# The way out of an expert block issued two blocks later, the ranking behind the first gather, and gated values in two small buffers

## The chip, the core and the metric

The kernel runs on one core of one Trainium2 chip. Its engines run side by side, each with its own queue in program order: TensorE (PE) multiplies, VectorE (DVE) and ScalarE (ACT) work element by element, GpSimd (POOL) does little here, SyncE (SP) issues the transfers. The metric is the device time of one execution in microseconds. Before the change it is 1520.44 us, the median of three runs (1520.12 to 1522.35).

## The reference

A two-layer encoder trunk on 256 tokens of width 1024, in float32. Each layer adds to the residual stream `h` a token mixer, a cross attention over 256 memory tokens, and a feed-forward part; layer 0 has a dense one of width 2816, layer 1 a mixture of eight experts of width 3584, of which each token takes two:

```python
logits = (xt @ w_router).astype(jnp.float32)
top_vals, top_idx = lax.top_k(logits, TOP_K)
top_w = jax.nn.softmax(top_vals, axis=-1)
combine = jnp.sum(jax.nn.one_hot(top_idx, N_EXPERTS, dtype=jnp.float32) * top_w[..., None], axis=1)
y = jnp.zeros_like(xt)
for e in range(N_EXPERTS):
    y = y + combine[:, e:e + 1] * swiglu(xt, w_gate[e], w_up[e], w_down[e])
```

with `swiglu(x) = (silu(x @ w_gate) * (x @ w_up)) @ w_down`. The expert weights are 352 MB, and every one of them is read once; that part takes more than half of the time.

## The kernel before, in words

**Weights.** They arrive in chunks of 1 MB (128 x 2048 float32), a chunk per DMA, into a buffer of the pool R (22 buffers of that size). Each chunk is split in two: ACT rounds it to `hi` (L196), DVE subtracts for `lo` (L197), both in R. Activations are split in the same way. A product is then three matmuls, hi·hi, hi·lo and lo·hi (in a small expert block two, since there the two halves of the activations stand side by side in one operand). The splits run up to four chunks ahead of PE, in five pairs of buffers; transfers are issued up to seven chunks ahead of the splits (`do_split`, `get`, `dma`, L160 to L209), but each must wait until its buffer is free.

**Expert blocks.** The tokens of an expert are gathered by a matmul with a one-hot matrix (`gather`: `pg` on DVE at L1132, the matmuls at L1147, ACT and DVE move the result to `xg` at L276 and L278). Eight experts stand in eight places, each cut into 7 blocks of 512 columns. Four places (0, 5, 6, 7) are large, with 128 slots for tokens; four are small, with 64; which expert stands where is decided on the chip by `sort`. A block has four steps: the gate product (two chunks), the value product (two chunks), the gated values, and the way out, `down` (two chunks, added to two PSUM banks `acc`). All these products are recorded at L1202. Large and small blocks alternate (`merged`), after three large ones and up to three small ones at the end: 28 pairs, a cycle of which spans seven.

**From value product to way out.** In a large block ACT applies SiLU to the gate product, DVE multiplies in the value product (`a`, L1246), PE turns the result by four transposes (L1228, `hidden`). In a small block ACT copies both products out, PE turns each (L1226), DVE multiplies (L1256). Then `parts` makes the two halves `hl` of the gated values: ACT the rounded one, DVE the rest (L1266). `down` reads them as the standing operand.

**Order.** There is no scheduler: the instructions stand in each engine's queue as the code issues them. `Run.blocks` issues for block i: its gate product, `hidden` of block i−1, its value product with `parts` of block i−1 in its middle, `gated`, and then the way out of block i−1. `chunks` lists the weight chunks in the order in which these steps take them. `later` holds small pieces (gather matmuls, adding a finished place to `h`) that are issued between the steps.

**The start of the experts.** `moe` gathers place 0 (`first`); after its first piece two splits, `weights` (the softmax of two) and `sort` (some twenty small DVE operations, L1027 to L1057) are issued, then the gather's other pieces. `sort` gives the numbers of the experts that stand in places 1 to 7, and their slots.

**Kept chunks.** The K product of layer 1's attention takes its weights partly from chunks that were loaded and split during layer 0's feed-forward part (`KEPT`, L423 to L434); a chunk holds two K blocks. The others come with the stream, split or not as the string `FULL` says; unsplit ones are multiplied at L461, one matmul of two passes, which the trace records as two.

Of the kernel before, what the change touches and what calls it, by code (L numbers as in the profile page):

```python
# [21 lines left out]
F32R = mybir.dt.float32r  # L22
# [7 lines left out]
P = 128  # L30
# [32 lines left out]
SPL = [(j * 512, min(512, FF - j * 512)) for j in range((FF + 511) // 512)]  # L63


KEPT = 3

R_BUFS = 22
M_BUFS = 8

SPLIT_BUFS, SPLIT_AHEAD = 3, 3
WIDE_BUFS, WIDE_AHEAD = 5, 8

WIDE_LOAD = 7

HALF = 64
SMALL = 4
LEAD = 3
# [4 lines left out]
def trunk(tc, x, xt_in, mem, mt_in, wa, wb, wc, wl0, wk1, wl1, wff, wmoe, cc, tk, moec, ident_d, gfin, out):  # L83
    nc = tc.nc
    PE, ACT, DVE, POOL = nc.tensor, nc.scalar, nc.vector, nc.gpsimd
    with contextlib.ExitStack() as c:
# [745 lines left out]
        def pe_later(n=1):  # L832
            for _ in range(n):
                if later:
                    later.pop(0)()
# [4 lines left out]
        def up(st, s, accs, mid=None):  # L840


            np_ = s.w // 128
            per = 1024 // s.w

            def part(i, wh, wl, t):
                for j in range(per):
                    k = i * per + j
                    w = slice(j * s.w, (j + 1) * s.w)
                    a, b = s.x(k, t)  # L850
                    mm3(accs[t][:, 0:s.w], a, b, wh[:, w], wl[:, w], k == 0, k == KC - 1)

            if mid:
                parts = st.many(np_)
                for t in range(NT):
                    for i in range(np_):
                        part(i, *parts[i], t)
                        if t == 0 and i == np_ // 2 - 1:
                            mid()
            else:  # L860
                for i in range(np_):
                    w = st.get()
                    for t in range(NT):
                        part(i, *w, t)
# [322 lines left out]
        class Block:  # L1187
# [7 lines left out]
            def product(self, x, out, items, first, last):  # L1195

                if self.small:
                    ops = [(x[:, f].rearrange("p i s -> p (i s)"), it[i]) for i in range(2) for f, *it in items]
                else:
                    ops = [(x[:, f, i], w) for f, wh, wl in items for i, w in ((0, wh), (0, wl), (1, wh))]  # L1200
                for i, (a, w) in enumerate(ops):
                    PE.matmul(out, a, w, start=first and i == 0, stop=last and i == len(ops) - 1)  # L1202

            def up(self, out, mid=None):
                for c in range(2):
                    if c and mid:
                        mid()
                    items = []
                    for i, (wh, wl) in enumerate(self.st.many(2)):
                        items += [(4 * c + 2 * i + q, wh[:, q * 512:(q + 1) * 512], wl[:, q * 512:(q + 1) * 512])  # L1210
                                  for q in range(2)]
                    self.product(self.place.xg, out, items, c == 0, c == 1)

            def copy(self, ps):
                m = M([P, 512], s="gu")
# [21 lines left out]
                    self.a = M([P, 512], s="a")  # L1237
                    ACT.activation(self.a, g, AF.Silu)  # L1238

            def value(self, mid=None):  # L1240
                u = mm()
                self.up(u, mid)
                if self.small:
                    self.u = self.copy(u)
                else:
                    DVE.tensor_tensor(self.a, u, self.a, op=OP.mult)  # L1246
# [12 lines left out]

            def parts(self):  # L1260
                n = self.place.n
                self.hl = (M if self.small else R)([P, 4, 2, n], F32R, s="hl")
                v = self.a.rearrange("p (f s) -> p f s", f=4)
                hi, lo = self.hl[:, :, 0], self.hl[:, :, 1]
                ACT.activation(hi, v, AF.Copy)
                DVE.tensor_tensor(lo, v, hi.bitcast(F32), op=OP.subtract)  # L1266

# [17 lines left out]
        class Run:  # L1285
# [14 lines left out]
            def blocks(self, st, steps, before):  # L1300

                fin = Final()
                prev = None
                todo = [Block(st, p, j) for p, j in steps]
                for i, b in enumerate(todo):
                    last = i == len(todo) - 1
                    if i in before:
                        before[i]()
                    if last:
                        fin.load()  # L1310
                    b.gate()
                    pe_later()
                    if prev:
                        prev.hidden()
                    pe_later()
                    b.value(prev and prev.parts)
                    pe_later()
                    b.gated()

                    def hidden():  # L1320
                        b.hidden()
                        b.parts()
                    if prev:
                        prev.down(hidden if last else None)
                    pe_later()
                    prev = b
                while later:
                    pe_later()
                table(AF.Sqrt)
                prev.down(end=lambda: fin.all(prev.place.part))  # L1330

        def merged():

# [7 lines left out]
        def chunks(order, at):  # L1341

            src = []
            for i, (p, j) in enumerate(order):
                src += [at(p, 6 * j + c) for c in range(4)]
                if i:
                    q, k = order[i - 1]
                    src += [at(q, 6 * k + c) for c in (4, 5)]
            q, k = order[-1]
            src += [at(q, 6 * k + c) for c in (4, 5)]  # L1350
            return [(a, 1024, (False, False)) for a in src]

        where = {}
# [12 lines left out]
        def moe(st, routed, weights, sort, combine):  # L1366
            slot, comb, slotp, combp, which, bases, nmax, r, saved = routed
            where["tile"] = which
            order = merged()
            run = Run(slotp, combp, r, saved)  # L1370
            places = [Place(run, p, 1 <= p <= SMALL) for p in range(NE)]

            places[0].run = Run(slot, comb, r, saved)
            st.wide = True
            first = places[0].gather()
            later.append(first.pop())
            later.append(combine)
            for i, f in enumerate(first):
                f()
                if i == 0:  # L1380
                    for _ in range(2):
                        st.do_split()
                    weights()
                    sort()
            st.ahead = WIDE_LOAD
            before = {}
            at = {x: i for i, x in enumerate(order)}

            def add(i, f):
                before.setdefault(i, []).append(f)  # L1390
            add(LEAD, run.save)
            for p in range(1, NE):
                add(max(1, at[p, 0] - 3), places[p].prepare)
            run.blocks(st, [(places[p], j) for p, j in order],
                       {i: lambda fs=fs: [f() for f in fs] for i, fs in before.items()})
# [70 lines left out]
        norm = mixer(1, st, kv1, norm, start1)  # L1466
        nxt = Norm(1, C_FFN, split=False)
        attention(1, st, kv1, norm, nxt)
        st.ahead = 6 * LEAD - 4
        routed, *pieces = route(nxt)  # L1470
        moe(st, routed, *pieces)

# [147 lines left out]
```

## Time and profile before

| what | value |
|---|---|
| median of three runs | 1520.44 us |
| profiled execution: time, span | 1520.13 us, 1518.4 us |
| PE busy | 1468.9 us, 97% |
| DVE busy, ACT busy | 1295.8 us, 85%; 1046.9 us, 69% |
| bytes moved, mean rate | 459 MB, 302 GB/s |
| expert chunks | 336 of 1 MB |

The experts begin at about 590 us and end with the span, and in this part the transfers run at 360 to 420 GB/s, so averages over the span say little about it. Stretches of it are read by themselves: "pair" is one large and one small block, about 30 us when nothing else is issued in it. The records of matmuls overlap: the start of one to the start of the next is what it costs PE, not its length. "Idle before" is what an engine waited just ahead of an instruction, with the instruction that released it.

### The profile page before, as it was taken

The page shows a single profiled execution, that of the slowest core. Times are in us where ns is not written, and L with a number is a line of the kernel's source. Part 1 is how long each engine was busy: PE and PEld are TensorE (multiplying, and loading weights), DVE is VectorE, ACT ScalarE, POOL GpSimd, SP SyncE. Part 2 cuts the span into 40 slices and gives each one's busy share as a digit, 9 for nine tenths or more (in the row PEclk, how much of TensorE's full clock was granted, in tenths as well). Part 3 has the DMA queues.
Part 4 walks back from the last instruction along what each step waited for, and adds up shares of the span by engine and source line. Part 5 has one row for each costly group of instructions (what it writes and reads, how often), then busy time and mean ns, then how long its engine had stood idle before and what let it go on. Part 6 is the DMA issues. An engine that isn't in the chain of part 4 may idle for free.

```text
span 1518.4 us, 20836 instructions
## 1 busy us (share of the span) xinstructions
PE 1468.9 (97%) x7773; PEld 1263.6 (83%) x7773; DVE 1295.8 (85%) x1498; ACT 1046.9 (69%) x1226; POOL 8.0 (1%) x23
## 2 busy tenths in 40 slices
PE   7999999999999998999999999999999999999996
PEld 7998988888999897888888778888777888777884
DVE  7988767555798867999998999998999998999996
ACT  7547574444653655788787878787878787878884
POOL 0000000000000001000000000000000000000000
PEclk9999999999999998999999999999999999999998
DMA  9625465544452547599999999999999999999991
GB/s 371 245 90 215 164 231 186 203 167 180 153 210 81 208 162 324 196 383 418 388 403 399 359 373 423 378 406 388 373 374 420 376 410 372 380 366 422 416 418 65
DMA packets 65327, 459.04 MB, mean 302 GB/s; under 512 B 7233, under 2 KB 7745, under 8 KB 11841
## 3 DMA queue, kind: packets, MB, share of 16 engines
q1 hardware_dynamic: 65216, 457.62, 75.9%
q8 instruction: 63, 1.03, 0.3%
q14 instruction: 48, 0.39, 0.1%
HBM read 456.55 MB, written 1.05 MB: 301 GB/s over the span
## 4 chain that ended last, share of the span: by engine, by line
PE 83%; DVE 8%; ACT 4%; issue 3%; DMA 0%; SPq 0%; DVEq 0%; ACTq 0%
PE mm L1202 26%; PE acc L1202 16%; PE mm L220 5%; PE mm L218 5%; PE mm L219 5%; DVE lo L197 5%; PE acc L219 3%; PE acc L220 3%; PE acc L218 3%; ACT hi L196 3%; PE z L219 2%; PE z L220 2%; PE z L218 2%; PE mm L461 2%; PE mm L490 2%
## 5 line engine op out<-in xcount | busy, mean ns | idle before, releaser
L197 DVE TENSOR_TENSOR lo<-w,hi 128x2048 fp32r<-128x2048 f32 (+3 forms) x504 | 943.6, 1913 | 57.5 <-ACT hi L196 50.6
L196 ACT ACTIVATE hi<-w 128x2048 fp32r<-128x2048 f32 (+3 forms) x504 | 795.0, 1616 | 108.8 <-DVE lo L197 36.5
L1202 PE MATMUL mm<-hi,xg 128*128 128x512 f32 x1344 | 409.9, 393 | 2.2 <-DVE xg L278 1.1
L1202 PEld LDWEIGHTS mm<-hi,xg 128*128 128x128 f32 x1344 | 250.6, 188 | 53.2 <-DVE xg L278 1.6
L1202 PE MATMUL mm<-lo,xg 128*128 128x512 f32 x896 | 294.5, 390 | 0.0
L1202 PE MATMUL acc<-hi,hl 128*128 128x512 f32 x672 | 219.1, 401 | 23.5 <-DVE hl L1266 23.5
L1202 PEld LDWEIGHTS mm<-lo,xg 128*128 128x128 f32 x896 | 168.3, 188 | 34.6
L1202 PEld LDWEIGHTS acc<-hi,hl 128*128 128x128 f32 x672 | 124.4, 189 | 60.5 <-DVE hl L1266 36.6
L1202 PE MATMUL acc<-lo,hl 128*128 128x512 f32 x448 | 157.4, 392 | 0.0
L1202 PEld LDWEIGHTS acc<-lo,hl 128*128 128x128 f32 x448 | 84.6, 189 | 17.0
L218 PE MATMUL z<-hi,xt 128*128 128x320 f32 (+1 forms) x256 | 78.4, 306 | 7.9 <-ACT xt L336 7.9
L219 PE MATMUL z<-lo,xt 128*128 128x320 f32 (+1 forms) x256 | 77.5, 303 | 0.1
L220 PE MATMUL z<-hi,xt 128*128 128x320 f32 (+1 forms) x256 | 77.5, 303 | 0.0
L546 DVE SCALAR_TENSOR_TENSOR ca<-ca,cct 128x256 f32<-128x256 f32 x180 | 77.1, 480 | 0.2
L218 PE MATMUL mm<-hi,xt 128*128 128x512 f32 (+1 forms) x192 | 71.8, 374 | 0.0
L220 PE MATMUL mm<-hi,xt 128*128 128x512 f32 (+1 forms) x192 | 71.4, 372 | 0.0
L219 PE MATMUL mm<-lo,xt 128*128 128x512 f32 (+1 forms) x192 | 71.3, 371 | 0.0
L1226 PEld LDWEIGHTS mm<-twice,gu 128*128 128x128 f32 x448 | 58.1, 191 | 3.9
L1238 ACT ACTIVATE a<-mm 128x512 f32<-128x512 f32 x28 | 16.7, 596 | 61.3 <-PE mm L1202 61.3
L1226 PE MATMUL mm<-twice,gu 128*128 128x64 f32 x448 | 56.1, 268 | 0.0
L218 PEld LDWEIGHTS z<-hi,xt 128*128 128x128 f32 x256 | 49.4, 193 | 8.0 <-ACT xt L336 7.9
L219 PEld LDWEIGHTS z<-lo,xt 128*128 128x128 f32 x256 | 49.4, 193 | 0.3 <-DVE lo L197 0.3
(284 smaller groups left out, 1929.7 us busy)
## 6 DMA issues: line engine op xcount, KB each, us to landing
w<-in_wmoe_dram SPq DMA_DIRECT2D x336, 1024.0 KB, 7.9
w<-in_wl_dram SPq DMA_DIRECT2D x39, 1024.0 KB, 4.9
w<-in_wff_dram SPq DMA_DIRECT2D x33, 1024.0 KB, 4.8
w<-in_wb_dram SPq DMA_DIRECT2D x8, 960.0 KB, 8.7
w<-in_wa_dram SPq DMA_DIRECT2D x5, 1024.0 KB, 6.0
w<-in_wc_dram SPq DMA_DIRECT2D x8, 640.0 KB, 5.1
tk<-in_tk_dram SPq DMA_DIRECT2D x2, 1024.0 KB, 10.9
mt<-in_mem_t_dram SPq DMA_DIRECT2D x2, 1024.0 KB, 11.8
```

The costliest lines, as they stand in the source:

```text
L196: ACT.activation(hi[:, ws], r, AF.Copy)
L197: DVE.tensor_tensor(lo[:, ws], r, hi[:, ws].bitcast(F32), op=OP.subtract)
L218: PE.matmul(ps, ah, bh, start=start, stop=False)
L219: PE.matmul(ps, ah, bl, start=False, stop=False)
L220: PE.matmul(ps, al, bh, start=False, stop=stop)
L461: PE.matmul(self.kps[:, d, :], w[:, ks], self.mt[:, k, :], start=k == 0, stop=k == KC - 1)
L490: PE.matmul(ps[:, t, :], self.mt[:, k, tok(t)], p_[:, w], start=k == 0, stop=k == KC - 1)
L546: return lambda: DVE.scalar_tensor_tensor(dst, src[:, k:k + S], w, dst, op0=OP.mult, op1=OP.add)
L1202: PE.matmul(out, a, w, start=first and i == 0, stop=last and i == len(ops) - 1)
L1226: PE.matmul(ps[:, f * n:(f + 1) * n], w, twice, start=True, stop=True)
L1238: ACT.activation(self.a, g, AF.Silu)
```

## The change

1. The order in `Run.blocks` and of the chunks in `chunks`: block i's gate product, `hidden` of block i−1, the way out of block i−2 with `parts` of block i−1 in its middle, block i's value product, `gated`. Two ways out are left at the end.
2. `sort` is issued behind all pieces of the first gather instead of behind the first one.
3. The halves of a large block's gated values stand in two buffers of the pool M instead of one of R. R has 21 buffers instead of 22, M (a quarter of the size) 12 instead of 8. Small blocks keep one M buffer.
4. Two K chunks are kept instead of three. By `FULL`, the two K blocks of the third, which now comes with the stream, are not split.
5. 14 instead of 16 chunks may be issued before the ranking (`6 * LEAD - 6`); they are those of place 0, which need no ranking. `PRESPLIT` names a number that stays 2.

Lines of the changed kernel are two higher (L1202 becomes L1204) and one higher from L1226 to L1246.

```diff
-KEPT = 3
-R_BUFS = 22
-M_BUFS = 8
+KEPT = 2
+R_BUFS = 21
+M_BUFS = 12
...
+PRESPLIT = 2
...
                 if self.small:
-                    ops = [(x[:, f].rearrange("p i s -> p (i s)"), it[i]) for i in range(2) for f, *it in items]
+                    ops = [(x[0][:, f].rearrange("p i s -> p (i s)"), it[i]) for i in range(2) for f, *it in items]
                 else:
-                    ops = [(x[:, f, i], w) for f, wh, wl in items for i, w in ((0, wh), (0, wl), (1, wh))]
+                    ops = [(x[i][:, f], w) for f, wh, wl in items for i, w in ((0, wh), (0, wl), (1, wh))]
...
             def parts(self):
                 n = self.place.n
-                self.hl = (M if self.small else R)([P, 4, 2, n], F32R, s="hl")
+                if self.small:
+                    t = M([P, 4, 2, n], F32R, s="hl")
+                    self.hl = t, None
+                    hi, lo = t[:, :, 0], t[:, :, 1]
+                else:
+                    hi, lo = self.hl = [M([P, 4, n], F32R, s="hl") for _ in range(2)]
                 v = self.a.rearrange("p (f s) -> p f s", f=4)
-                hi, lo = self.hl[:, :, 0], self.hl[:, :, 1]
...
                     b.gate()
                     pe_later()
-                    if prev:
-                        prev.hidden()
+                    if i:
+                        todo[i - 1].hidden()
+                    if i > 1:
+                        pe_later()
+                        todo[i - 2].down(todo[i - 1].parts)
+                    elif i:
+                        todo[i - 1].parts()
                     pe_later()
-                    b.value(prev and prev.parts)
+                    b.value()
                     pe_later()
                     b.gated()
-
-                    def hidden():
-                        b.hidden()
-                        b.parts()
-                    if prev:
-                        prev.down(hidden if last else None)
-                    pe_later()
-                    prev = b
+                b.hidden()
+                todo[-2].down(b.parts)
                 while later:
                     pe_later()
                 table(AF.Sqrt)
-                prev.down(end=lambda: fin.all(prev.place.part))
+                b.down(end=lambda: fin.all(b.place.part))
...
             for i, (p, j) in enumerate(order):
-                src += [at(p, 6 * j + c) for c in range(4)]
-                if i:
-                    q, k = order[i - 1]
+                src += [at(p, 6 * j + c) for c in (0, 1)]
+                if i > 1:
+                    q, k = order[i - 2]
                     src += [at(q, 6 * k + c) for c in (4, 5)]
-            q, k = order[-1]
-            src += [at(q, 6 * k + c) for c in (4, 5)]
+                src += [at(p, 6 * j + c) for c in (2, 3)]
+            for q, k in order[-2:]:
+                src += [at(q, 6 * k + c) for c in (4, 5)]
...
                 if i == 0:
-                    for _ in range(2):
+                    for _ in range(PRESPLIT):
                         st.do_split()
                     weights()
-                    sort()
+            sort()
...
-        st.ahead = 6 * LEAD - 4
+        st.ahead = 6 * LEAD - 6
```

On PE, around a small block in the middle of the experts (`xg_7552` before, `xg_7484` after are its tokens). Before: its gate product, the turn of the large block ahead of it (`a_7865`), its value product, the turn of its own gate (`gu_7976`), and the way out of the large block just turned (`hl_8006`):

```order
L1202 MATMUL mm_7947<-hi_7874,xg_7552 128x512 x4
...
L1202 MATMUL mm_7947<-lo_7896,xg_7552 128x512 x4
...
L1228 MATMUL mm_7982<-ident,a_7865 128x128 x4
...
L1202 MATMUL mm_7991<-hi_7914,xg_7552 128x512 x4
...
L1202 MATMUL mm_7991<-lo_7929,xg_7552 128x512 x4
...
L1226 MATMUL mm_8029<-twice,gu_7976 128x64 x4
L1202 MATMUL acc_7508<-hi_7948,hl_8006 128x512
L1202 MATMUL acc_7508<-lo_7949,hl_8006 128x512
```

After: the same steps, with the way out of the block before the turned one (`hl_7826`) between the turn and the value product:

```order
L1204 MATMUL mm_7885<-hi_7808,xg_7484 128x512 x4
...
L1204 MATMUL mm_7885<-lo_7830,xg_7484 128x512 x4
L1229 MATMUL mm_7916<-ident,a_7800 128x128 x4
L1204 MATMUL acc_6417<-hi_7848,hl_7826 128x512 x2
...
L1204 MATMUL acc_6418<-lo_7867,hl_7826 128x512 x2
L1204 MATMUL mm_7958<-hi_7886,xg_7484 128x512 x4
...
L1204 MATMUL mm_7958<-lo_7901,xg_7484 128x512 x4
...
L1227 MATMUL mm_7993<-twice,gu_7914 128x64 x4
L1204 MATMUL mm_8000<-hi_7921,xg_6845 128x512
```

The way out that follows the value product is gone from there; the next block's gate product (`mm_8000`) follows at once, and the turned block's own way out comes a block later.

On DVE, at the start of the experts. Before: two splits, the ranking (its first and last operation), the moves of place 0's tokens, three splits:

```order
L197 TENSOR_TENSOR lo_5751<-w_5557,hi_5750 128x2048
L1027 COPY t_5766<-mm_5695 128x8
...
L1057 CAST nmax<-t_5790 128x1
L278 SCALAR_TENSOR_TENSOR xg_5721<-mm_5796,cct,xg_5721 128x128 x4
L278 SCALAR_TENSOR_TENSOR xg_5721<-mm_5813,cct,xg_5721 128x128 x4
L197 TENSOR_TENSOR lo_5832<-w_5726,hi_5831 128x2048
```

After:

```order
L199 TENSOR_TENSOR lo_5709<-w_5519,hi_5708 128x2048
L280 SCALAR_TENSOR_TENSOR xg_5683<-mm_5724,cct,xg_5683 128x128 x4
L280 SCALAR_TENSOR_TENSOR xg_5683<-mm_5741,cct,xg_5683 128x128 x4
L1029 COPY t_5758<-mm_5657 128x8
...
L1059 CAST nmax<-t_5782 128x1
L199 TENSOR_TENSOR lo_5790<-w_5688,hi_5789 128x2048
```

The ranking has moved behind the eight moves and stands ahead of the third split.

## Rows read from the trace of the kernel before

**Rows 1.** Page, part 1: busy us, share of the span, instructions.

```profile
PE 1468.9 (97%) x7773; PEld 1263.6 (83%) x7773; DVE 1295.8 (85%) x1498; ACT 1046.9 (69%) x1226; POOL 8.0 (1%) x23
```

**Rows 2.** Page, part 5: busy us, mean ns, idle time before and its releaser.

```profile
L197 DVE TENSOR_TENSOR lo<-w,hi 128x2048 fp32r<-128x2048 f32 (+3 forms) x504 | 943.6, 1913 | 57.5 <-ACT hi L196 50.6
...
L1202 PE MATMUL acc<-hi,hl 128*128 128x512 f32 x672 | 219.1, 401 | 23.5 <-DVE hl L1266 23.5
```

**Rows 3.** Waits of PE, 620 to 1462 us: total us, times, longest.

```profile
PE acc L1202 <- DVE hl L1266: 20.3, 25, 1.6
```

**Rows 4.** Timeline of PE, 1453 to 1463.6 us: start, length, tile, count, idle before.

```profile
1453.25 1.07 PE L1202 MATMUL mm<-hi,xg 128*128 128x512 f32 x4
...
1456.88 0.60 PE L1228 MATMUL mm<-ident,a 128*128 128x128 f32 x4
...
1462.12 0.40 PE L1202 MATMUL acc<-lo,hl 128*128 128x512 f32 x1
1463.01 0.73 PE L1202 MATMUL acc<-hi,hl 128*128 128x512 f32 x2 [0.49 <-DVE hl L1266]
```

**Rows 5.** Timeline of DVE, 1450 to 1463 us.

```profile
1450.66 0.69 DVE L1246 TENSOR_TENSOR a<-mm,a 128x512 f32<-128x512 f32 x1
1451.26 11.09 DVE L197 TENSOR_TENSOR lo<-w,hi 128x2048 fp32r<-128x2048 f32 x5
1462.27 0.68 DVE L1266 TENSOR_TENSOR hl<-mm,hl 128x512 fp32r<-128x512 f32 x1
```

**Rows 6.** Timeline of PE after its wait at 1339.75 us.

```profile
1339.75 1.04 PE L1202 MATMUL acc<-hi,hl 128*128 128x512 f32 x2 [1.64 <-DVE hl L1266]
...
1343.50 0.63 PE L1202 MATMUL acc<-hi,hl 128*128 128x512 f32 x2
```

**Rows 7.** Windows: length, busy PE, PEld, DVE, ACT, POOL, PEclk, DMA share, GB/s.

```profile
629.50:660.90 31.40, 31.16 (x145) 25.63 (x144) 29.18 (x17) 26.18 (x19) 0.00 (x0) 1.00 0.96 366
755.20:981.50 226.30, 220.11 (x1066) 182.84 (x1064) 212.62 (x149) 180.94 (x149) 0.00 (x0) 1.00 0.97 390
1340.00:1344.00 4.00, 4.00 (x12) 3.10 (x12) 4.00 (x3) 0.06 (x1) 0.00 (x0) 0.57 0.40 170
1371.20:1401.50 30.30, 29.79 (x141) 24.62 (x140) 28.47 (x17) 24.74 (x19) 0.00 (x0) 1.00 1.01 421
1462.10:1478.50 16.40, 15.91 (x78) 13.11 (x76) 16.38 (x13) 13.33 (x13) 0.00 (x0) 1.00 1.01 422
```

**Rows 8.** Page, part 6: expert chunks, KB each, median us to landing.

```profile
w<-in_wmoe_dram SPq DMA_DIRECT2D x336, 1024.0 KB, 7.9
```

**Rows 9.** Waits of the DMA queue of SyncE, 620 to 1462 us.

```profile
SPq L170 <- PE mm L1202: 374.2, 134, 8.0
```

**Rows 10.** Timeline of DVE and ACT around the ranking and the first gather.

```profile
599.01 0.15 DVE L1027 COPY t<-mm 128x8 f32<-128x8 f32 x1
...
601.07 2.15 ACT L276 ACTIVATE xg<-mm,cct 128x128 fp32r<-128x128 f32 x8
...
602.95 2.15 DVE L278 SCALAR_TENSOR_TENSOR xg<-mm,cct,xg 128x128 fp32r<-128x128 f32 x8
...
618.95 0.53 DVE L1132 TENSOR_SCALAR pg<-mct,slotp,t 128x64 f32<-128x64 f32 x2
```

**Rows 11.** Timeline of PE there.

```profile
603.35 0.73 PE L1202 MATMUL mm<-hi,xg 128*128 128x512 f32 x2 [1.15 <-DVE xg L278]
...
619.60 3.68 PE L1147 MATMUL mm<-pg,h 128*128 128x64 f32 x32
```

**Rows 12.** Timeline of PE in layer 1's K product.

```profile
451.69 3.72 PE L461 MATMUL mm<-mt,w 128*128 128x256 f32 x16
455.06 0.47 PE L218 MATMUL mm<-ms,khi 128*128 128x256 f32 x1
...
456.20 0.28 PE L220 MATMUL mm<-ms,klo 128*128 128x256 f32 x1
456.32 0.28 PE L218 MATMUL mm<-ms,khi 128*128 128x256 f32 x1
```

More of the change, by code (lines that the diff above doesn't have):

```diff
@@ L1197, in product, with up @@
                 if self.small:
-                    ops = [(x[:, f].rearrange("p i s -> p (i s)"), it[i]) for i in range(2) for f, *it in items]
+                    ops = [(x[0][:, f].rearrange("p i s -> p (i s)"), it[i]) for i in range(2) for f, *it in items]
                 else:
-                    ops = [(x[:, f, i], w) for f, wh, wl in items for i, w in ((0, wh), (0, wl), (1, wh))]
+                    ops = [(x[i][:, f], w) for f, wh, wl in items for i, w in ((0, wh), (0, wl), (1, wh))]
                 for i, (a, w) in enumerate(ops):
                     PE.matmul(out, a, w, start=first and i == 0, stop=last and i == len(ops) - 1)
-            def up(self, out, mid=None):
+            def up(self, out):
                 for c in range(2):
-                    if c and mid:
-                        mid()
                     items = []
@@ L1211, in up @@
                                   for q in range(2)]
-                    self.product(self.place.xg, out, items, c == 0, c == 1)
+                    xg = self.place.xg
+                    self.product((xg, None) if self.small else (xg[:, :, 0], xg[:, :, 1]), out, items, c == 0, c == 1)
             def copy(self, ps):
@@ L1238, in gate, with value @@
                     ACT.activation(self.a, g, AF.Silu)
-            def value(self, mid=None):
+            def value(self):
                 u = mm()
-                self.up(u, mid)
+                self.up(u)
                 if self.small:
@@ L1302, in blocks @@
                 fin = Final()
-                prev = None
                 todo = [Block(st, p, j) for p, j in steps]
                 for i, b in enumerate(todo):
-                    last = i == len(todo) - 1
                     if i in before:
                         before[i]()
-                    if last:
+                    if i == len(todo) - 1:
                         fin.load()
```

## The prediction

> **What bounds the kernel now.** The page comes first: TensorE (PE) is busy for 97% of the span [rows 1], so time can only come from its gaps or from its matmuls' number and pace. Of the costly groups, only the matmuls of the way out, `acc<-hi,hl`, have much idle time ahead of them: 23.5 us, all put down to the subtraction `hl` of VectorE (DVE) at L1266 [rows 2]. The waits of PE, cut to the expert blocks between 620 and 1462 us, name nothing else: 25 waits, 20.3 us [rows 3]. So three questions remain: what one such wait costs, what would be late next, and what the other edits cost.
>
> The timeline of one pair of blocks answers the first. Four queued 128x512 matmuls take 1.07 us and a single one shows 0.39 (0.40 here), so they follow one another every (1.07 − 0.39)/3 = 0.227 us, and 0.165 of a record is the pipeline's tail [rows 4]. Around a wait the starts at 1462.12 and 1463.01 stand 0.89 us apart: lost are 0.89 − 0.23 = 0.66, where the bracket says 0.49. A wait of the list therefore costs its idle time and about 0.165 more. Its cause stands in the order: the gated values of the block before are turned only after the next block's gate product, ScalarE (ACT) and DVE make their two parts in the middle of its value product, DVE ends `hl` at 1462.95 [rows 5], and the first matmul that reads it is due at 1462.35.
>
> What would be late next: in a cycle of seven pairs of blocks (755.20 to 981.50) the span is 226.3 us. DVE is busy for 212.6 and the transfers run at 390 GB/s. The bare pair at 1371.20 runs at 421 GB/s, the stretch at 629.50, where the transfers wait for free buffers, at 366 [rows 7]. One chunk is 1.0486 MB: 2.49 us at 421 GB/s, so 84 chunks of a cycle need 209 us and the 12 of a pair 29.9. SyncE's queue waits mostly for PE to release a buffer [rows 9], so a transfer starts when a buffer comes free, and lands 7.9 us after its issue in the median [rows 8].
>
> **The change part by part.** *The way out two blocks later.* Every matmul, split and transfer of a block stays; the same instructions stand in another order. PE now runs the way out of block i−2 between the gate and the value product of block i, and the parts of block i−1 are made in its middle. They are first read after the rest of that way out, the value product and the next gate product: at least 8 + 16 + 16 matmuls, 40 x 0.227 = 9.1 us, against the 0.68 of `hl` and a split or two of 11.09/5 = 2.2 in front of it [rows 5]. So these waits go: 20.3 + 25 x 0.165 = 24.4 us. The cycle of seven pairs loses its share of them, 24.4 x 226.3/(1462 − 620) = 6.6, and comes to 219.7 us. DVE's 212.6 is then 97% of it and the transfers' 209 are 95%: both still fit, barely. In a bare pair the page gives 30.3 us of span against 29.79 of PE [rows 7]. Without its waits the pair needs about 29.6 of PE, and the transfers 29.9.
>
> *What is late next.* (a) The turn of a large block (L1228) needs DVE's product `a`. Now a second half of a way out and a gate product lie between: `a` starts at 1450.66 and ends at 1451.35 [rows 5], the turn starts at 1456.88 [rows 4], 5.5 us of slack. The 32 matmuls between value product and turn began 32 x 0.227 = 7.3 us before it, at 1449.6. Afterwards only the 16 of a small gate lie between, 3.6 us: the turn would come at 1453.2 and 1.9 us of slack are left, a little under one split. I take no wait here; where DVE runs one split late it costs 0.3 to 0.5 a time, 28 times at most, so 0 to 14 us. (b) The pool R loses one of 22 buffers for good, and a large block's `hl` had held one only part of the time. Read off the order, a transfer mostly took the buffer of 11 chunks earlier and now takes that of 10: transfers start about 2.5 us later against the work. In bare pairs they then bind at 29.9 against 29.6; for some six of them, and for small losses where DVE has no slack (16.38 of 16.40 us at 1462.10 [rows 7]), I add 2.0 us. The bounds: −0 (all hidden), and 12 if half of the removed waits come back as waits for splits.
>
> Two M buffers of a quarter of an R buffer hold the parts of a large block; 12 M buffers at three or four a block last three blocks, and the parts live for one and a half. I cost that at nothing, with PE's queue as the cover; a wait of ACT for such a buffer would delay splits, and belongs to (b).
>
> *The clock.* After the wait of 1.64 us at 1339.75 PE is slow [rows 6]: from 1339.75 to 1343.50 nine matmuls take 3.75 us, 0.42 each, instead of 9 x 0.227 and the start of a fresh run, 2.2 in all. The window 1340 to 1344 shows a granted clock of 0.57 [rows 7], so most of it at the lower level, 1.2 GHz. The difference, 1.6 us, goes with that wait.
>
> *The ranking behind the first gather.* Now DVE sorts the experts from 599.01 until just before 602.95 (3.9 us) while ACT loads a table and only then moves the gathered tokens from 601.07 on; DVE's own eight moves `xg` follow at 602.95 and PE waits 1.15 us for them at 603.35 [rows 10, 11]. Changed, DVE moves `xg` when ACT's first four are done, 601.07 + 4 x 0.27 = 602.2, ends at 604.4 instead of 605.1, and PE's wait falls by 0.7. But the sort no longer lies in idle time: it ends at 608.3, and the splits, the combine step and the rows `pg` of the next place's gather are queued behind it on DVE, 608.3 − 605.1 = 3.2 us later, less the 0.3 that DVE waited: 2.9. `pg` ended at 619.48, right ahead of the gather at 619.60, which PE now reaches at 618.9 and which can start only at 622.4. So 619.60 becomes 622.3: +2.7 us, with a new wait of about 3.3 us. I take +2.6 (bounds −0.7, if the splits are scheduled around it, and +4). SyncE needs the ranks only for its first dynamic chunk, behind 14 static ones.
>
> After that wait the clock may drop as it did at 1339.75: by that row I add 1.6 us, with bounds 0 (a cycle with seven or eight such waits stands at 1.00 [rows 7]) and 3.2 (all 32 gather matmuls half as fast, 0.1 us each).
>
> The Trainium skill (TensorE: Matmul & The Clock Gate, "Why this matters for your kernels") says that an idle gap between bursts of matmuls takes TensorE back to its lower clock. By that rule the new wait brings a dip for certain, and the removal of 25 short ones saves only what [rows 6] shows; the trace agrees at one of the 25.
>
> *One K chunk less kept.* Two K blocks of layer 1 are now made by matmuls on unsplit weights like those at 451.69: 16 records in 455.06 − 451.69 = 3.37 us, 0.21 each [rows 12], two records a matmul. 16 such matmuls are 32 records, 6.7 us; 48 split ones at 0.12 [rows 12], 5.8 us, go. PE has no gap there: +1.0 us (0.5 to 1.5). One chunk is loaded later and its split leaves ACT and DVE earlier; they are not late there.
>
> *The tail.* From 1462 on DVE is full [rows 7], so the last waits (23.5 − 20.3 = 3.2 us) mostly stay: −0.3 (0 to −1.5).
>
> The sum against the profiled run of 1520.13 us (span 1518.4), 0.3 below the median of 1520.44: 1520.1 − 24.4 − 1.6 + 2.0 + 2.6 + 1.6 + 1.0 − 0.3 = 1501.0 us.
>
> **The rivals.** *DVE and the transfers give a good part back.* For it: 97% and 95% of the new cycle, and a buffer fewer. Against it: PE waits for no split in the whole window [rows 3]. Half of the 24.4 comes back: 1501 − 2 + 12 = 1511 us.
>
> *The wait moves to the turn,* (a) at its upper end: 1515 us. For it: 5.5 us of slack become 2.0; against it: in the pair shown `a` starts 0.9 us after the end of its product (1449.6 and 0.165), not a split late.
>
> *Slower: the shorter look-ahead starves the stream.* With ten chunks instead of eleven the queue falls back to what 629.50 shows, 366 GB/s [rows 7] or 2.87 us a chunk, where a transfer is issued only as one lands. All 84 chunks so: 241 us a cycle, against 226.3; two thirds so and the rest at 2.49: 230 us, 3.8 more than before. A stream of 56 blocks is four cycles: 1520 + 15 + 1 = 1536 us. It decides as soon as the mean falls under 88.1 MB/226.3 us = 389 GB/s, which is about where it is now (390) because of PE's pace.
>
> The Trainium skill (DMA: Bandwidth & Descriptors, "Where 436 GB/s comes from") holds that from HBM to SBUF the HBM's share of about 358 GB/s binds. By that figure a cycle's transfers take an estimated 246 us and no reordering on PE could pay; the 421 GB/s of [rows 7] speak against it on this one core, and I give it no chance of its own.
>
> *No change:* if the `hl` waits only stand for DVE's lateness, then each reappears elsewhere on PE, 1518 to 1522 us.
>
> **How the numbers follow.** Forecast 0.60 (1496 to 1507, with single terms at their bounds), better still 0.06 (dip, transfers and start all at their low ends, 1493), DVE and transfers 0.17, the turn 0.07, no change 0.04, slower 0.06. The range 1494 to 1514 leaves out the slower case, no change, and part of the two above. Faster by over 0.2% (about what a measurement here tells from none, 3 us) 0.90, within it 0.04, slower 0.06.
>
> **What the changed profile would show.** Right: no wait of `acc` for `hl` before 1440 us; one new PE wait of about 3 us at the gather some 20 us after the first expert matmul; cycles of seven pairs of about 220 us; 32 unsplit records more in layer 1's K. Wrong if PE waits for `lo` or `a` in the blocks, if DMA runs under 395 GB/s in a cycle, or if the sort's end moves the gather by less than 1 us.

## The result, and the profile after

The changed kernel takes 1514.72 us, the median of six executions, beside 1522.11 us for the kernel before. One of the six (2099.60 us, mean granted clock 0.656) was disturbed and is left out of the comparison; the other five run from 1510.55 to 1518.28 us, with 1513.38 in the middle. The ratio is 0.9948, 95% interval [0.9927, 0.9969]: faster by 7.9 us, where 19 were forecast. The median of the six lies 0.7 us outside the forecast range, the middle one of the five 0.6 us inside it; what was missed is the gain. The profiled execution is the fastest, 1510.55 us with a span of 1508.7, so the two traces differ by 9.7 us.

First the page of the changed kernel, the lines that answer to [rows 1, 2] (busy us, mean ns | idle before, releaser):

```profile
PE 1469.5 (97%) x7757; PEld 1270.9 (84%) x7757; DVE 1293.9 (86%) x1496; ACT 1043.2 (69%) x1224; POOL 7.9 (1%) x23
...
L199 DVE TENSOR_TENSOR lo<-w,hi 128x2048 fp32r<-128x2048 f32 (+3 forms) x504 | 946.4, 1917 | 56.9 <-ACT hi L198 37.8
...
L1204 PE MATMUL acc<-hi,hl 128*128 128x512 f32 x672 | 217.4, 398 | 0.0
```

The idle time ahead of `acc<-hi,hl` is gone, 23.5 to 0.0 us. Its place is taken by others; the waits of PE from 570 to 1500 us (total, times, longest), to set against [rows 3]:

```profile
PE mm L1149 <- DVE pg L1134: 8.2, 5, 3.1
PE mm L1179 <- DVE y L273: 4.5, 5, 1.2
...
PE mm L1227 <- ACT gu L1217: 2.0, 1, 2.0
...
PE mm L1229 <- DVE a L1247: 0.5, 3, 0.2
PE mm L1204 <- DVE xg L280: 0.4, 1, 0.4
```

All are DVE or ACT being late with small operations: the one-hot rows `pg` of a gather, the parts `y` of a finished place, a copy `gu`, the product `a`. Some 14.5 us of them are new (8.2 less 0.7 that the first gather had waited before, 4.5, 2.0 and 0.5). Between 620 and 1462 us none of these stood in the list before. The windows show what they cost (length, busy PE, PEld, DVE, ACT, POOL, PEclk, DMA share, GB/s):

```profile
624.00:634.00 10.00, 10.00 (x44) 9.41 (x44) 6.68 (x12) 3.95 (x11) 0.00 (x0) 0.52 0.24 99
745.30:966.70 221.40, 218.53 (x1065) 183.31 (x1065) 212.58 (x148) 180.59 (x148) 0.00 (x0) 1.00 0.99 399
1484.00:1488.00 4.00, 4.00 (x13) 3.19 (x13) 3.57 (x3) 0.40 (x1) 0.00 (x0) 0.57 0.02 6
```

The cycle of seven pairs, measured between the starts of the same gate product, takes 221.4 us, where [rows 7] has 226.3 and the prediction 219.7. And there are two new stretches at the lower clock, 624 to 634 (0.52) and 1484 to 1488 (0.57). From 640 to 1480 no stretch is below 1 any more; before, 1340 to 1344 was.

The start, against [rows 10, 11]; first the timeline of PE (start, length, tile, count, idle before):

```profile
604.07 0.73 PE L1204 MATMUL mm<-hi,xg 128*128 128x512 f32 x2 [0.42 <-DVE xg L280]
...
620.11 0.39 PE L1204 MATMUL mm<-hi,xg 128*128 128x512 f32 x1
623.64 6.38 PE L1149 MATMUL mm<-pg,h 128*128 128x64 f32 x32 [3.14 <-DVE pg L1134]
629.81 1.06 PE L1229 MATMUL mm<-ident,a 128*128 128x128 f32 x4
```

And that of DVE, with the ranking's first operation at L1029:

```profile
603.66 2.16 DVE L280 SCALAR_TENSOR_TENSOR xg<-mm,cct,xg 128x128 fp32r<-128x128 f32 x8 [3.13 <-ACT xg L278]
605.74 0.15 DVE L1029 COPY t<-mm 128x8 f32<-128x8 f32 x1
...
609.70 6.70 DVE L199 TENSOR_TENSOR lo<-w,hi 128x2048 fp32r<-128x2048 f32 x3
...
623.18 0.53 DVE L1134 TENSOR_SCALAR pg<-mct,slotp,t 128x64 f32<-128x64 f32 x2
```

PE's wait for `xg` falls from 1.15 to 0.42 us, the ranking now fills DVE from 605.74 to 609.70, and `pg` starts at 623.18 instead of 618.95. PE waits 3.14 us for it, and the 32 gather matmuls then take 629.81 − 623.64 = 6.17 us, where they took 623.12 − 619.60 = 3.52 before. The instruction behind them in the timeline of PE before:

```profile
623.12 0.61 PE L1228 MATMUL mm<-ident,a 128*128 128x128 f32 x4
```

Where the 9.7 us of the two traces come from, with the same points of both programs laid on each other (the new order has one way out less behind it at the same gate product, 24 or 16 matmuls of 0.227 us, which is added):

| stretch | forecast, us | measured, us |
|---|---|---|
| to the first expert product (601.47 before, 602.91 after) | +1.0 | +1.4 |
| to the third block's gate product (635.2; 638.2 + 5.45) | +4.2 | +7.0 |
| to the fourth pair (742.5; 745.3 + 3.63) and through three cycles (1453.3; 1438.9 + 3.63) | −24.0 | −19.2 |
| the end | −0.3 | +1.1 |
| sum | −19.1 | −9.7 |

### The profile page after: what moved, and what is told of

It reads as the page before. It is cut to its first block, busy times and chain, and to the rows that moved or that the text cites. A ratio compares the mean times of both kernels' runs of the same rounds, so it can differ in the third digit from the quotient of the medians.

```text
span 1508.7 us, 20807 instructions
## 1 busy us (share of the span) xinstructions
PE 1469.5 (97%) x7757; PEld 1270.9 (84%) x7757; DVE 1293.9 (86%) x1496; ACT 1043.2 (69%) x1224; POOL 7.9 (1%) x23
## 4 chain that ended last, share of the span: by engine, by line
PE 90%; DVE 4%; issue 2%; ACT 2%; DMA 1%; POOL 0%; SPq 0%; DVEq 0%; ACTq 0%; POOLq 0%
PE mm L1204 31%; PE acc L1204 16%; PE mm L220 5%; PE mm L222 5%; PE mm L221 5%; PE mm L1227 3%; PE acc L221 3%; PE acc L222 3%; PE acc L220 3%; PE mm L463 3%; PE z L221 2%; PE z L222 2%; PE z L220 2%; DVE lo L199 2%; PE mm L1149 2%
## 5 line engine op out<-in xcount | busy, mean ns | idle before, releaser
L1204 PE MATMUL mm<-hi,xg 128*128 128x512 f32 x1344 | 405.4, 393 | 1.6 <-ACT xg L278 1.2
L1204 PEld LDWEIGHTS mm<-hi,xg 128*128 128x128 f32 x1344 | 253.0, 189 | 53.7 <-ACT xg L278 1.4
L1204 PE MATMUL mm<-lo,xg 128*128 128x512 f32 x896 | 295.3, 391 | 0.0
L1204 PE MATMUL acc<-hi,hl 128*128 128x512 f32 x672 | 217.4, 398 | 0.0
L1204 PEld LDWEIGHTS mm<-lo,xg 128*128 128x128 f32 x896 | 168.8, 188 | 34.1
L1204 PE MATMUL acc<-lo,hl 128*128 128x512 f32 x448 | 157.7, 393 | 0.0
L1204 PEld LDWEIGHTS acc<-hi,hl 128*128 128x128 f32 x672 | 125.2, 189 | 24.4
L1204 PEld LDWEIGHTS acc<-lo,hl 128*128 128x128 f32 x448 | 84.8, 189 | 17.4
L1227 PE MATMUL mm<-twice,gu 128*128 128x64 f32 x448 | 56.2, 268 | 2.0 <-ACT gu L1217 2.0
L220 PEld LDWEIGHTS z<-hi,xt 128*128 128x128 f32 x256 | 49.7, 194 | 7.2 <-ACT xt L338 7.0
L222 PEld LDWEIGHTS z<-hi,xt 128*128 128x128 f32 x256 | 49.5, 193 | 0.0
```

The costliest lines, as they stand in the source:

```text
L220: PE.matmul(ps, ah, bh, start=start, stop=False)
L222: PE.matmul(ps, al, bh, start=False, stop=stop)
L1227: PE.matmul(ps[:, f * n:(f + 1) * n], w, twice, start=True, stop=True)
```

## The experiments

Three theories were open. *Look-ahead:* with one buffer of R less, splits wait for buffers, DVE falls behind, and the small operations queued behind those splits come late. *Load:* DVE at 97% and the transfers at 95% of the forecast cycle simply hold it. *Queue order:* each late operation only stands in a bad place of DVE's queue. Beside them, the start: whether the clock falls because of the wait for `pg`.

| kernel | median, us | ratio to before [95%] | cycle, us |
|---|---|---|---|
| before | 1522.1 to 1523.7 | 1 | 226.3 |
| changed | 1514.72 | 0.9948 [0.9927, 0.9969] | 221.4 |
| e1: ranking put back | 1507.46 | 0.9894 [0.9879, 0.9908] | 221.4 |
| e2: before, ranking moved alone | 1532.11 | 1.0045 [1.0031, 1.0059] | 227.9 |
| e3: changed, `pg` a block earlier | 1512.01 | 0.9919 [0.9906, 0.9931] | 222.1 |
| e7: e1, `pg` earlier, `y` read later | 1504.02 | 0.9874 [0.9858, 0.9890] | 221.9 |
| e10: e1 with 22 and 8 buffers | 1496.89 | 0.9819 [0.9799, 0.9839] | 218.6 |
| e11: e1 with 20 R buffers | 1535.53 | 1.0087 [1.0067, 1.0107] | 231.8 |
| e9: before with 21, 12 and two kept chunks | 1534.79 | 1.0073 [1.0053, 1.0092] | 228.4 |
| e13: e1, splits three chunks ahead | 1495.03 | 0.9810 [0.9791, 0.9829] | 218.2 |
| e17: before, splits three chunks ahead | 1523.04 | 0.9994 [0.9981, 1.0007] | 225.9 |
| e12: e10 with the parts in R | 1496.61 | 0.9806 [0.9785, 0.9826] | 218.6 |
| e18: e10 with three kept chunks | 1492.87 | 0.9794 [0.9775, 0.9812] | 218.7 |
| e16: e18, splits three chunks ahead | 1492.89 | 0.9797 [0.9779, 0.9815] | 218.3 |

**e1, the ranking put back.**

```diff
                     weights()
-            sort()
+                    sort()
```

> The changed kernel with one edit undone: the ranking stands again behind the first piece of the first gather. Theory: in the changed kernel the ranking delays DVE, so PE waits 3.1 us for pg at the gather of place 1, the clock falls to its lower level behind that wait, and the 32 gather matmuls and the 12 to 15 after them run at half pace (6.17 instead of 3.52 us, and 2.1 us more). Without it: 3.3 + 4.8 us go, 0.6 of the wait for xg comes back, so 7.5 us off the profiled 1510.6: 1503 us, and the runs spread less than 1510.6 to 1518.3 if that dip is what varies. Rival: the dip comes from the routing stretch at 588 to 600 us, not from the wait; then only 2.7 us go (1508) and the lower clock after 620 stays.

The profiled run took 1501.56 us, 9.0 less; the two ratios differ by 0.0054, 8 us. The wait for `pg` at the start and the clock's fall are gone, while the cycle is as in the changed kernel (windows, columns as above):

```profile
620.00:640.00 20.00, 20.00 (x110) 17.17 (x109) 18.22 (x18) 15.32 (x20) 0.00 (x0) 1.00 0.78 290
736.40:957.80 221.40, 218.54 (x1066) 183.25 (x1065) 212.55 (x148) 180.65 (x148) 0.00 (x0) 1.00 0.98 399
```

At 620 to 640 PEclk is 1.00. The theory holds for the start. Of the 9.0 us, 1.4 stand between the two traces before the ranking is reached (PE begins the gather of place 0 at 594.09 instead of 595.52), so they are not the edit's; 7.5 remain. The spread did not fall: 1501.56 to 1508.52.

**e2, the ranking moved in the kernel before.** The same lines moved the other way.

> The kernel before with one edit alone: the ranking behind all pieces of the first gather. Theory: a wait of about 3 us for pg at the gather of place 1 (619.6 before), the clock falls behind it, and the time rises by 2.6 to 7.5 us, to 1523 (no dip) or 1528 (dip). Rival: without the new order DVE catches up by the gather, and the time stays within 1 us of 1520.4 or falls by the 0.6 us of the shorter wait for xg.

Slower by 0.45%, 7 us in timed runs. The waits of PE:

```profile
PE acc L1202 <- DVE hl L1266: 21.5, 26, 1.6
PE mm L1147 <- DVE pg L1132: 3.8, 2, 3.1
```

A wait for `pg` of 3.1 us is there in the old order as well, so it belongs to this edit. The clock falls behind it here too (0.50 from 624 to 632 us), as it does in e3, which keeps the moved ranking (0.50 from 626 to 632). Part of the loss lies elsewhere and is the clock. Four stretches in this trace's cycles are below 1, each behind a wait for `hl` of 1.39 to 1.65 us; the trace of the kernel before has nearly the same waits and one such stretch. The four windows:

```profile
894.00:899.00 5.00, 4.40 (x12) 3.52 (x13) 5.00 (x4) 1.14 (x2) 0.00 (x0) 0.66 0.51 215
1090.00:1094.00 4.00, 4.00 (x12) 3.15 (x11) 4.00 (x3) 2.42 (x2) 0.00 (x0) 0.57 1.01 424
1124.00:1128.00 4.00, 3.96 (x10) 3.13 (x11) 4.00 (x3) 0.09 (x1) 0.00 (x0) 0.57 0.53 221
1352.00:1356.00 4.00, 4.00 (x11) 3.20 (x12) 4.00 (x3) 0.12 (x2) 0.00 (x0) 0.61 0.51 217
```

**e3, the one-hot rows earlier.**

```diff
-                add(max(1, at[p, 0] - 3), places[p].prepare)
+                i = max(1, at[p, 0] - 3)
+                add(i if p == 1 else i - 1, places[p].early)
+                add(i, places[p].prepare)
```

> The changed kernel, with the one-hot rows pg of places 2 to 7 issued one block earlier than their gather's matmuls. Theory: three waits for pg of 1.47 us idle (1.63 from start to start) go, one in each cycle of seven pairs, 4.9 us off the profiled run: 1505.7, cycle 219.7 instead of 221.3 us. Rival: DVE and the transfers are what limits a cycle; then the lateness shows elsewhere (at y, a, or a split) and the cycle stays at 221 us, the time at 1510 to 1511.

The rival's number: the cycle is 222.1 us. The wait for `pg` is gone from it, and the turn now waits for `a` (waits of PE in one cycle):

```profile
PE mm L1231 <- DVE a L1249: 2.3, 3, 1.1
PE mm L1181 <- DVE y L273: 1.2, 1, 1.2
```

The median is nevertheless 3 us better, not by the cycle: these runs have a mean clock of 0.990 to 0.992, those of the changed kernel 0.984 to 0.989.

**e7, three edits.** e1, e3, and one more slot ahead of the four pieces that read `y`:

```diff
-                later.append(lambda: None)
+                later.extend([lambda: None] * 2)
```

> The changed kernel with three edits: the ranking back behind the first piece, pg one block earlier, and the four pieces that add a finished place to h one piece slot later. Theory: the waits for pg (3.1 and three of 1.47) and for y (three of 1.22 and one of 0.6) go, with the clock dip at 624: 7.5 + 4.9 + 4.9, from 1510.6 to about 1493 us, cycle of seven pairs 218.3 us. Rival: DVE at 97% and the transfers hold the cycle near 221 us; then only the start's 7.5 go, 1503 us.

Again the rival: the cycle is 221.9, and everything that `pg` and `y` had waited is now waited for `a`. The window of a cycle:

```profile
736.40:958.30 221.90, 218.48 (x1065) 183.14 (x1064) 212.09 (x148) 179.65 (x148) 0.00 (x0) 1.00 0.98 398
```

The waits of PE in it:

```profile
PE mm L1231 <- DVE a L1249: 3.4, 4, 1.1
```

So the place of a single operation is not the cause; DVE is late as a whole. Where it becomes late is seen in the changed kernel's own trace, ahead of its wait for `pg`. The timeline of ACT:

```profile
808.15 5.52 ACT L198 ACTIVATE hi<-w 128x2048 fp32r<-128x2048 f32 x3 [2.26 <-PE mm L1204]
```

DVE:

```profile
810.10 2.29 DVE L199 TENSOR_TENSOR lo<-w,hi 128x2048 fp32r<-128x2048 f32 x1 [1.82 <-ACT hi L198]
...
824.95 4.49 DVE L199 TENSOR_TENSOR lo<-w,hi 128x2048 fp32r<-128x2048 f32 x2
829.35 0.54 DVE L1134 TENSOR_SCALAR pg<-mct,slotp,t 128x64 f32<-128x64 f32 x2
```

PE:

```profile
827.86 0.39 PE L1204 MATMUL mm<-hi,xg 128*128 128x512 f32 x1
829.72 2.56 PE L1149 MATMUL mm<-pg,hs 128*128 128x64 f32 x21 [1.47 <-DVE pg L1134]
```

ACT waits 2.26 us for a buffer that PE must free, so DVE waits 1.82 us for that `hi`. It is the buffer and not the chunk that comes late: a matmul that read a `lo` ends at 808.1, just ahead of ACT's start, and the last transfer had landed at 806.4. From 810.10 on DVE has no gap until `pg` at 829.35, for which PE has waited 1.47 us: what was lost at 810 is paid at 829. This is one place's reading; the next runs test it.

**e10, the buffers of before.** The new order and the parts of large blocks in M, but:

```diff
-R_BUFS = 21
-M_BUFS = 12
+R_BUFS = 22
+M_BUFS = 8
```

> The changed kernel with the ranking back behind the first piece (profiled 1501.6 us, cycle of seven pairs 221.4), and with the buffers of before: 22 of R and 8 of M, the parts of large blocks still in M. Theory: a cycle is held by the look-ahead; ACT waits 19 us a cycle for buffers that PE frees, DVE then is late with the small operations behind the split. With one buffer more these waits shrink and those of PE for pg, y and a (3.4 us a cycle) mostly go: cycle 218 to 219.5, profiled 1491 to 1496. Rival: DVE at 96% of the cycle is the limit and the buffers are none: 221.4 and 1501. Second rival: 8 M buffers are too few for parts that live longer, ACT waits for them, and the cycle becomes longer than 221.4.

The first theory's number: 218.6 us, and of the waits one of 0.4 is left. The window of a cycle:

```profile
739.10:957.70 218.60, 218.19 (x1065) 183.31 (x1064) 212.42 (x149) 181.10 (x149) 0.00 (x0) 1.00 0.99 403
```

The waits of PE in it:

```profile
PE mm L1179 <- DVE y L273: 0.4, 1, 0.4
```

DVE is busy for 212.42 of 218.60, 97%, and the transfers run at 403 GB/s; neither holds the cycle. Eight M buffers are enough. **e11, one buffer of R less than the changed kernel** (`R_BUFS = 20`), goes the other way:

> The changed kernel with the ranking back behind the first piece, and one buffer of R less (20). Theory (look-ahead): transfers and splits start 2.5 us later against the work, the waits of PE for pg, y and a grow, cycle 224 us or more instead of 221.4, 1510 us or more. Rival (DVE's load): 221.4 and 1501 to 1502.

The window of a cycle:

```profile
740.00:971.80 231.80, 224.06 (x1066) 187.47 (x1065) 213.06 (x148) 180.17 (x149) 0.00 (x0) 0.98 0.94 381
```

The waits of PE in it:

```profile
PE mm L1229 <- DVE a L1247: 3.2, 3, 1.1
PE mm L1149 <- DVE pg L1134: 2.7, 2, 1.3
PE mm L1179 <- DVE y L273: 1.8, 1, 1.8
```

The cycle grows to 231.8 us and the rate falls to 381 GB/s. The time, 1535.5 us, is that of the forecast's slower rival (1536), but the way is not the rival's: between 620 and 1450 us no wait of ACT, DVE or PE is put down to a transfer. PE waits 7.7 us of the cycle for the same late small operations (2.9 in e1), and the granted clock is 0.98 where e1 has 1.00. ACT's waits for buffers that PE frees, 620 to 1450 us (total, times, longest), in e11:

```profile
ACT hi L198 <- PE mm L1204: 115.2, 69, 4.5
```

In e1, with 21 buffers:

```profile
ACT hi L198 <- PE mm L1204: 56.2, 58, 2.6
```

In e10:

```profile
ACT hi L198 <- PE mm L1204: 48.0, 67, 1.3
```

Their sum hardly tells 21 from 22 buffers; the longest one does, 4.5, 2.6 and 1.3 us. In a cycle of e1 three waits of ACT for `hi` are over 1.5 us (2.61, 2.26 and 1.89), in one of e10 none. That fits the reading at 808: the few long waits make DVE late, and the many short ones leave PE a wait of 0.4 us a cycle.

**e9, the buffers alone in the old order** (`KEPT = 2`, `R_BUFS = 21`, `M_BUFS = 12`):

> The kernel before with the buffers of the changed one alone: 21 of R, 12 of M, two kept K chunks; order, ranking and the place of the parts as before. Theory (look-ahead): in the old order too a buffer less makes DVE later, the waits for hl grow, cycle 227 to 229 instead of 226.3, and K costs 1.0 to 1.5: 1523 to 1530. Rival: buffers cost nothing in the old order, only K does: 1521.1 to 1521.6.

The window of a cycle:

```profile
749.40:977.80 228.40, 220.06 (x1066) 182.85 (x1065) 213.76 (x149) 182.01 (x150) 0.00 (x0) 1.00 0.96 387
```

Slower by 0.73%, 11 us: more than the first theory expected. In the old order the same buffers cost about as much as in the new (0.75% between e1 and e10), here with the 1.15 us of the K chunk among it, and the place of the cost is `hl`: from 590 us on PE waits 33.5 us for it, where the kernel before has 23.5.

**e13, splits three chunks ahead.** On e1, with 21 and 12 buffers:

```diff
-WIDE_BUFS, WIDE_AHEAD = 5, 8
+WIDE_BUFS, WIDE_AHEAD = 5, 6
```

> The changed kernel with the ranking back behind the first piece, and the splits issued three chunks ahead of PE instead of four. Theory (look-ahead): it takes no buffer away but uses one pair less of split ones; the small operations stand one split earlier in the queue of DVE, so the waits for pg, y and a go, but PE now waits for lo where DVE had been late: cycle 219 to 224. Rival (queue order alone makes pg, y and a late): cycle 218 to 218.5, profiled 1491, and no wait for lo.

Here the rival's cycle came, and my expectation of waits for `lo` did not (window of a cycle):

```profile
739.40:957.60 218.20, 217.95 (x1065) 183.40 (x1064) 212.03 (x149) 179.55 (x149) 0.00 (x0) 1.00 0.99 407
```

A split takes two buffers where a raw chunk takes one. Asked for one chunk later, it hardly stands waiting any more at the head of the queues of ACT and DVE with the small operations behind it; ACT's waits, to set against e1's 56.2 us above:

```profile
ACT hi L198 <- PE mm L1204: 19.7, 25, 1.5
```

e10 removes the waits of PE with a buffer more and the splits where they were, e13 with the buffers as they were and later splits. That makes buffers and queue order one cause: a split issued before its buffers are free. Whether the pair less in use or the later place in the queue does it was not separated. **e17, the same number in the kernel before,** was to show whether the old waits had that root too:

> The kernel before with one number changed: splits are issued three chunks ahead of PE instead of four. Theory (a split that waits for a buffer holds up what is queued behind it on ACT and DVE): the waits for hl in the old order have the same root, they fall from 23.5 us to under 10, the cycle from 226.3 to 219 to 222 us, the time from 1520 to 1500 to 1507. Rival: in the old order hl is late because it is made only half a value product ahead of its use; then the waits stay over 15 us and the time over 1512.

They have not. The time is the same, and the waits are too (PE, 590 us to the end):

```profile
PE acc L1202 <- DVE hl L1266: 23.4, 29, 1.8
```

ACT's own waits for buffers that PE frees did fall, from 43.4 us before to 9.4 (620 to 1450 us), and `hl` came no earlier. In the old order `hl` was late because it is made half a value product ahead of its use; that needed the new order.

**e12, the parts of large blocks in R,** with 22 and 8 buffers (`self.hl` a tile of R again):

> The changed kernel with the ranking back behind the first piece, the parts of large blocks in one buffer of R as before, and 22 and 8 buffers. Against e10 (parts in M, cycle 218.6) one R buffer is taken while a large block's parts live, which is about one and a half blocks of every two. Theory: that is as good as a buffer lost most of the time; cycle 220 to 222, profiled 1498 to 1503. Rival: the buffer is free when the splits need it; 218.6 and 1494 to 1497.

The rival: 218.6 us as in e10. The two small buffers gave nothing that the R buffer, held for a while, did not. Paying for them with a buffer for good is what cost. **e18, three kept chunks** (`KEPT = 3` on e10), and **e16, that with splits three chunks ahead:**

> e10 (22 and 8 buffers, ranking back) with three kept K chunks as before. Theory: the K product of layer 1 is 1.0 to 1.5 us shorter and nothing else changes: PE reaches the gather of place 0 at 594.1 us instead of 595.4, the cycle stays 218.6, median 1494 to 1496. Rival: PE was waiting for something else there, no change: 1497.

> e18 with the splits three chunks ahead instead of four: the new order, the parts of large blocks in M, and everything else as before the change. Theory: no wait of PE for DVE is left in the cycles, 218.0 to 218.3 us, median 1491 to 1494, the fastest of all. Rival: with 22 buffers nothing is left for the shorter look-ahead to give (e10's waits were 1.4 us in all), 1494 to 1496 as e18.

e18 is 4 us faster than e10 by the medians, with intervals that overlap. The K product itself, from its first to its last record, takes 23.22 us with three chunks (before, e18) and 24.37 with two (changed, e10): 1.15 us. The rest is not explained by it. e16 equals e18: with 22 buffers a shorter look-ahead gives nothing more. Both are faster than the changed kernel by 1.5%, and e16's cycle has hardly a wait left. The window:

```profile
736.60:954.90 218.30, 218.04 (x1066) 183.42 (x1065) 211.98 (x149) 179.40 (x148) 0.00 (x0) 1.00 0.99 405
```

The waits of PE from 620 to 1500 us:

```profile
PE mm L1227 <- ACT gu L1217: 1.4, 1, 1.4
PE mm L1179 <- DVE y L273: 1.0, 4, 0.3
PE acc L1204 <- DVE hl L1271: 0.6, 1, 0.6
```

## Why the prediction was wrong

*The waits for `hl`: right.* They went, and with the buffers restored they are all gain: the stretch from 742.5 to 1453.3, 710.8 us before, takes 1424.5 − 739.1 = 685.4 in e10. That is 25.4 us, of which the dip at 1340 is 1.6; with the 2.0 that the changed kernel gains ahead of 742.5 it makes 27.4, where 24.4 + 1.6 = 26.0 were forecast.

*The look-ahead, step (b): the term that was mis-sized.* I added 2.0 us for one R buffer less. In the changed kernel the cycle stands 2.8 us over e10's and 3.2 over e13's. Over the whole stretch (745.3 to 1438.9) it takes 693.6 us, e10 takes 685.4 and e13 684.3 (739.37 to 1423.63): the term measured 8.2 to 9.3 us, and by the medians 0.75% (11 us) between e1 and e10. I counted what a late transfer costs in a bare pair (29.9 against 29.6) and took only PE's queue and the transfers as the things that wait. ACT's waits were named for the small M buffers only. Not counted was that a split which waits for its R buffers holds up both queues behind it, and that DVE, at 97%, had not made up the 1.8 us of 810 when `pg` was due 19 us later. The slack of one `a` (1.9 us) was worked out for a DVE that is on time; and what PE then waited for, `pg` at three later gathers (1.47 us each) and `y` (up to 1.2), stands in no term of the sum and not among its signs of being wrong, which name waits for `lo` and `a`.

*The rival "DVE and the transfers give a good part back"* came near in size (1511), by one of the two grounds it gives. The load of DVE and the transfers is refuted: e13 and e16 run DVE at 97% and the transfers at 405 to 407 GB/s without the waits. The other ground, a buffer fewer, is what e10 and e11 bear out, though not as waits of PE for splits. *The rival of the turn* is real as a place: in e3, e7 and e11 it is `a` that is waited for, 1.08 us at a time; as a cause of its own it is refuted. *The slower rival* did not come; its time does with one buffer less than this change took (e11), by ACT's waits and not by transfers issued as others land.

*The ranking: the wait right, the clock wrong.* Forecast were a wait of 3.3 us and 0.7 back at `xg`; measured 3.14 and 0.73. For the clock behind it I took 1.6 us, from a place where nine matmuls ran slow, with 3.2 as the upper bound. It stayed low for the whole gather and the matmuls behind it until 634.5: 2.65 and about 2.2 us, 4.8. In all the edit costs 7.5 us of trace, where 4.2 were forecast (e1 has its third block's gate product at 629.3 instead of 638.2, and of these 8.9 us 1.4 stand before the ranking), and 8 us of median. The Trainium skill (TensorE: Matmul & The Clock Gate, "Why this matters for your kernels") says that an idle gap between bursts of matmuls takes the clock down; the traces agree at each of the three waits of about 3.1 us (changed kernel, e2, e3), and I gave the rule too little weight against the row.

*K:* +1.0 forecast, +1.15 measured; the +1.4 of the table to the first expert product has the scatter of the start in it (e1, with the same two chunks kept, is there at 601.49). *The tail:* the waits of 3.2 us became one of 1.97 for `gu` and one of 0.6 for `y`, with a stretch at the lower clock behind them (1484 to 1488), +1.1 instead of −0.3. *Trace and median:* the trace of the changed kernel is its fastest run; the others go to 1518.28 us as their mean granted clock falls from 0.989 to 0.984. The sum was made against one execution, and gave no term for that.

## What to carry to other kernels

When an order is loosened so that one wait goes, ask which buffers the looser order takes, and count them by who stands in a queue behind the instruction that waits for them: here one buffer of 22 cost 8.2 us of the 25.4 that the removed waits gave. If moving a late operation only moves the wait, look upstream for the one long wait of the engine that feeds it; where buffers are short, fewer instructions issued ahead can be faster than more (e13; not with 22 buffers, e16). An operation that lies in a gap of its engine is free only there: behind the gap it delays all that follows.

## What the runs showed of the hardware

The clock falls behind some waits of PE and not behind others of the same length: with six waits for `hl` of 1.36 to 1.65 us each between 640 and 1480 us, the traces of the kernel before and of e17 have one stretch at the lower level behind them, that of e2 four; e9 has seven such waits of 1.37 to 2.07 us and two stretches. Behind the wait of about 3.1 us for `pg` it fell in all three traces that have one (changed kernel, e2, e3). Executions of one program differ in their mean clock and with it in time: 1510.55 us at 0.989 and 1518.28 at 0.984 for the changed kernel, 1501.56 at 0.993 and 1508.52 at 0.989 for e1. Where the clock fell in the slower executions is not on record, since only one of each kernel was traced. That shorter waits make the times scatter less is not shown: e13, e16 and e18, with short waits alone in the cycles, lie within 3 us each, but e10 and e12, with waits as short, run over 3.5 and 4.5 us, and e3, with longer ones, over 2.3.
